# Two output products of a hybrid decoder layer by Strassen's method

## The chip, the cores and the metric

The kernel runs on one core of a Trainium2 chip. TensorE (PE) multiplies, VectorE (DVE), ScalarE (ACT) and GpSimd (POOL) do the rest, SyncE (SP) issues transfers. The metric is the device time of one execution in microseconds.

## What is computed

One layer over 512 tokens of 1024 channels, in float32: a SwiGLU FFN, a token mixer, a cross-attention into 256 memory tokens, and another FFN. Each is added to a scaled `h` and normalised. Cut to what matters here:

```python
def _swiglu(h, w_in, w_out):
    gate, up = jnp.split(h @ w_in, 2, axis=-1)
    return (jax.nn.silu(gate) * up) @ w_out          # w_out 2816 x 1024

def _parallel_mixer(h, w_in, lb, gnorm, pool_w, pool_scale, w_out):
    ...                                              # 4 HGRN2 heads -> o, 4 pooled groups -> p, each (.., 512, 512)
    merged = jnp.concatenate([o, p], axis=-1)
    return merged @ w_out                            # w_out 1024 x 1024

def _memory_attention(h, mem, wq, wk, wv, wo):
    ...                                              # 4 heads of 256
    o = jnp.einsum('bhsm,bmhd->bshd', p, v).reshape(b_, s_, D_MODEL)
    return o @ wo                                    # wo 1024 x 1024

h = _layernorm(ALPHA * h + 0.5 * _swiglu(h, w_ffn1_in, w_ffn1_out), ln1_g, ln1_b)
h = _layernorm(ALPHA * h + _parallel_mixer(h, ...), ln2_g, ln2_b)
h = _layernorm(ALPHA * h + _memory_attention(h, mem, ...), ln3_g, ln3_b)
h = _layernorm(ALPHA * h + 0.5 * _swiglu(h, w_ffn2_in, w_ffn2_out), ln4_g, ln4_b)
```

## The kernel before

**Float32 in three products.** Each operand of a product is split into a high part (a cast to fp32r) and a low part (the rest). `split` (L67, L68) does this: ACT casts, DVE subtracts. PE then runs high x high, high x low, low x high into one PSUM bank. `wblock` loads a block of weights (128 x 1024 float32, 512 KB: two contraction tiles of 512 output columns) into one of seven `raw` slots through SP's queue and splits it into `whi_` and `wlo_` (seven slots of tag `q` in all) or, for blocks that are kept, into one `ws_` tile.

**The two products in question.** `out_gemm` computes `merged @ w_out` (names `mo`, weights `wmixo`) and `o @ wo` (names `xo`). It goes over two halves of 512 output columns; in each, four weight blocks times four token tiles (128 tokens) times two contraction tiles times three parts. So 192 matmuls of 128x128 by 128x512 a product (L226, L227, L228), into a bank for each token tile. When a bank is done, DVE adds it to `alpha * h` (L243) and takes statistics (L246); in the second half the layer norm of that token tile follows (`ln_tile`: L173, L175, `rstd` on POOL L177, four DVE passes over half a tile each L180, L183), and `transpose_h` lets PE turn the normalised tile (`trh`, L195) and splits the turned tile into the next product's operand (`moT`, `xoT`). The bank of `trh` is one of two.

Their left sides come in already split: the gated heads of the mixer (`og`, L887) are split into `mg` for each of four stretches of 128 tokens, the pooled groups in `pool_out` (L735), the attention's outputs `po` in `values` into `oT`.

**The FFNs' second products** use `strassen_gemm`: one level of Strassen's method, with 2x2 blocks (two halves of tokens, two halves of the first 20 of 22 contraction tiles, two halves of output columns); seven products instead of eight. A product is `left` (split of a left quarter or of a combination of quarters), five weight blocks (`right`), 60 matmuls in `block` (L356) for two token tiles, and one to four additions of its banks `u`, `v`, `w` to `h` (`add`: L367 with the scale of `h`, L370 without). The combinations of left quarters are made by `combine` on DVE (L339). The combinations of right quarters (`t1` to `t4`) are made in DRAM by POOL's DMA queue: `Sums.copy` copies a block (L284), `Sums.add` adds another to it in flight (L293). `spread` issues 40 such actions for the second FFN behind 50 weight blocks, each behind a tiny POOL instruction (`seen`, L302) that reads the block's high part and so sets the time.

**Order.** Each engine runs its instructions in a written order, which a scheduler fixes when the kernel is built; an instruction that waits holds up all behind it on its engine. Behind the mixing product PE has keys (`pk`) and values (`vm`) of the memory to compute, which need no `h`; behind the attention product it starts the second FFN (`f2p`), which needs `xoT`.

Of the kernel before, what the change touches and what calls it, by code (L numbers as in the profile page):

```python
# [16 lines left out]
P = 128  # L17
S = 512
# [16 lines left out]
def layer_kernel(ctx: ExitStack, tc: tile.TileContext, a, out):  # L35
# [173 lines left out]
    def out_gemm(wsrc, nkt, act, alpha, g, b, eps, name, final=False, order=None, stay=4, ys=None, pre=None):  # L209
        nb = nkt // 2  # L210
        order = list(range(nb)) if order is None else order
        tiles = None
        stats = [st.tile([P, 2, 6], F32, tag=f"stats{t}", name=f"stats{t}", bufs=1) for t in range(NT)]
        for hf in range(2):
            ps = [None] * NT
            head = nb - (2 if hf == 0 else stay)

            def part(t, i, w):
                if ps[t] is None:
                    ps[t] = mm_ps(f"{name}ps{hf}{t}")  # L220
                hi, lo = w
                for j in range(2):
                    ah, al = act(order[i] * 2 + j)
                    tsl = slice(t * P, (t + 1) * P)
                    wh, wl = hi[:, j * 512:(j + 1) * 512], lo[:, j * 512:(j + 1) * 512]
                    nc.tensor.matmul(ps[t], ah[:, tsl], wh, start=i == 0 and j == 0, stop=False)  # L226
                    nc.tensor.matmul(ps[t], ah[:, tsl], wl, start=False, stop=False)  # L227
                    nc.tensor.matmul(ps[t], al[:, tsl], wh, start=False, stop=i == nb - 1 and j == 1)  # L228

            for i in range(head):  # L230
                w = wblock(wsrc[hf, order[i]], f"{name}{hf}_{i}")
                for t in range(NT):
                    part(t, i, w)
            ws = [wblock(wsrc[hf, order[i]], f"{name}{hf}_{i}", stay=hf == 1 and i < head + 3) for i in range(head, nb)]
            if hf == 1:
                GB = ln_bcast(g, b)
                if pre is not None:
                    pre()
            for t in range(NT):
                for i, w in enumerate(ws):  # L240
                    part(t, head + i, w)
                sl = slice(hf * 512, hf * 512 + 512)
                nc.vector.scalar_tensor_tensor(  # L243
                    out=h[t][:, sl], in0=h[t][:, sl], scalar=float(alpha), in1=ps[t],
                    op0=ALU.mult, op1=ALU.add)
                nc.vector.bn_stats(stats[t][:, hf, :], h[t][:, sl])  # L246
                if hf == 1:
                    ln_tile(t, stats[t], GB, eps)
                    if final:
                        for q in range(2):  # L250
                            nc.sync.dma_start(out[t * P:(t + 1) * P, q * 512:(q + 1) * 512], h[t][:, q * 512:(q + 1) * 512])
                    else:
                        if t == 0:
                            tiles = [quarter(f"{name}T{q}") if ys is not None else b8([P, 2, 2, S], F32R, f"{name}T{q}")
                                     for q in range(4)]
                        transpose_h(t, tiles, ys)
        if final:
            return None
        if ys is not None:
            return tiles  # L260
        return [(tiles[k // 2][:, k % 2, 0, :], tiles[k // 2][:, k % 2, 1, :]) for k in range(KT)]

    KB1, KB2 = [0, 1, 4, 5, 8], [2, 3, 6, 7, 9]
    NB = len(KB1)

    class Sums:


        def __init__(self, wsrc, name):
            self.w, self.name, self.T = wsrc, name, {}
            self.copies = [(p, b) for b in range(NB) for p in ("t1", "t3", "t2", "t4")]
            self.adds = list(self.copies)

        def copy(self, behind, of=("t1", "t3", "t2", "t4"), engine=None):

            todo = [c for c in self.copies if c[0] in of]
            if todo:
                p, b = todo[0]  # L280
                self.copies.remove(todo[0])
                T = self.T[p, b] = scr.tile([P, 1024], F32, name=f"{self.name}{p}{b}")
                with tc.issue_after(behind):
                    (engine or nc.sync).dma_start(T, self.w[p in ("t3", "t2"), (KB2 if p in ("t2", "t4") else KB1)[b]])  # L284

        def add(self, behind):

            if self.adds and self.adds[0] in self.T:
                p, b = self.adds.pop(0)
                x = {"t1": lambda: self.w[1, KB1[b]], "t3": lambda: self.w[1, KB2[b]],  # L290
                     "t2": lambda: self.T["t1", b], "t4": lambda: self.T["t2", b]}[p]()
                with tc.issue_after(behind):
                    nc.gpsimd.dma_start(self.T[p, b], x, accum_op=ALU.add, max_dma_last_dim=8192)  # L293

        def spread(self, hi, over, count=[0]):

            total = 8 * NB
            n0, n1 = (total * (count[0] + i) // over for i in range(2))
            count[0] += 1
            for n in range(n0, min(n1, total)):  # L300
                seen = st.tile([P, 1], F32, tag="seen", name="seen")
                ins = nc.gpsimd.tensor_tensor(out=seen, in0=hi[:, 0:1].bitcast(F32), in1=mhalf[:, 0:1], op=ALU.mult).ins  # L302
                if self.copies and (n % 2 == 0 or n < 4):
                    self.copy(ins, engine=nc.gpsimd)
                else:
                    self.add(ins)

        def step(self, q, n):
# [5 lines left out]
            for _ in range(3 if n < 4 else 2):  # L314
                self.copy(ins, engine=nc.gpsimd)

    def strassen_gemm(wsrc, gt, S_, alpha, g, b, eps, name, final, pre):
        tiles = None
        stats = [st.tile([P, 2, 6], F32, tag=f"stats{t}", name=f"stats{t}", bufs=1) for t in range(NT)]
        lo, hi = slice(0, 256), slice(256, 512)  # L320
        quarter_ = {n: [gt[i][:, :, sl], gt[i + 2][:, :, sl], gt[4][:, i:i + 2, sl]]
                    for n, i, sl in (("a11", 0, lo), ("a12", 1, lo), ("a21", 0, hi), ("a22", 1, hi))}
        for n, i, sl in (("a12", 2, lo), ("a22", 2, hi)):
            quarter_[n][2] = gt[4][:, i:i + 2, sl]
# [12 lines left out]
        def combine(o, x, y, op):  # L337
            for i in range(3):
                nc.vector.tensor_tensor(out=quarter_[o][i], in0=quarter_[x][i], in1=quarter_[y][i], op=op)  # L339

        def right(p, stay=0):

            direct = {"b11": (0, KB1), "b21": (0, KB2), "b22": (1, KB2)}
            for i in range(NB):
# [14 lines left out]
        def product(T, p, ps, opens):  # L359
            for i, w in enumerate(right(p)):  # L360
                for t in range(2):
                    block(t, i, w, T, ps[t], opens, False)
# [12 lines left out]
        s1 = b8([P, 2, 4, 256], F32, f"{name}s1")  # L375
        s1_ = sm.tile([P, 2, 256], F32, tag="s1", name=f"{name}s1_", bufs=2)
        quarter_["s1"] = [s1[:, 0], s1[:, 1], s1_]
# [15 lines left out]
        product(L, "b21", w, True)  # L393
        combine("a12", "a12", "a11", ALU.add)
        L = left("a12")

        T = b8([P, 2, 2, S], F32R, f"{name}gs")
        split(gt[5][:, :2, :], T[:, :, 0, :], T[:, :, 1, :])
        gs = [[(T[:, k, 0, sl], T[:, k, 1, sl]) for k in range(2)] for sl in (lo, hi)]
        product(L, "b22", v, False)  # L400
# [665 lines left out]
```

## Time and profile before

| what | value |
|---|---|
| median of 3 runs | 1042.48 us (1042.39 to 1042.53) |
| profiled execution | 1043.13 us, span 1041.4 us |
| PE busy | 1025.7 us (98%) |
| DVE busy | 825.4 us (79%) |
| ACT busy | 504.3 us (48%) |
| POOL busy | 95.0 us (9%) |
| mean granted clock | 0.997 |

A row of instructions gives start, busy time, engine, line, operation and output<-inputs, shape and count; a bracket tells how long the engine was idle before it and what released it. A group has no start, and gives after the bar busy time and the mean ns of one, then idle time before them. A row of a stretch gives its bounds, its length and the busy time of PE, of the weight loads, DVE, ACT and POOL (with counts), then the granted TensorE clock, the share of the DMA engines and GB/s. Matmuls are pipelined, so that their durations overlap: what one costs is the step to the next start.

### The profile page before, as it was taken

The page shows a single profiled execution, that of the slowest core. Times are in us where ns is not written, and L with a number is a line of the kernel's source. Part 1 is how long each engine was busy: PE and PEld are TensorE (multiplying, and loading weights), DVE is VectorE, ACT ScalarE, POOL GpSimd, SP SyncE. Part 2 cuts the span into 40 slices and gives each one's busy share as a digit, 9 for nine tenths or more (in the row PEclk, how much of TensorE's full clock was granted, in tenths as well). Part 3 has the DMA queues.
Part 4 walks back from the last instruction along what each step waited for, and adds up shares of the span by engine and source line. Part 5 has one row for each costly group of instructions (what it writes and reads, how often), then busy time and mean ns, then how long its engine had stood idle before and what let it go on. Part 6 is the DMA issues. An engine that isn't in the chain of part 4 may idle for free. (4 is left out here: it accounts for less than half of the span.)

```text
span 1041.4 us, 17704 instructions
## 1 busy us (share of the span) xinstructions
PE 1025.7 (98%) x6910; PEld 929.4 (89%) x6910; DVE 825.4 (79%) x1334; ACT 504.3 (48%) x857; POOL 95.0 (9%) x167
## 2 busy tenths in 40 slices
PE   9999999999999999999999999999999999999996
PEld 7999999998887888879888988889999999988884
DVE  6999888789898545786786356589988888889795
ACT  5656555566554331334324345226555555566530
POOL 0112211200000111102303110010000000000000
PEclk9999999999999999999999999999999999999998
DMA  9377786585665446553929871403233332436751
GB/s 364 143 236 230 222 254 212 148 247 158 216 192 182 142 155 169 148 168 82 292 72 314 273 162 41 141 22 107 97 101 122 103 101 65 139 102 202 235 189 41
DMA packets 43300, 171.59 MB, mean 165 GB/s; under 512 B 6096, under 2 KB 7376, under 8 KB 40016
## 3 DMA queue, kind: packets, MB, share of 16 engines
q1 hardware_dynamic: 38592, 128.25, 36.9%
q0 software_dynamic: 4480, 41.95, 15.9%
q8 instruction: 54, 0.88, 0.3%
q10 hardware_dynamic: 144, 0.26, 0.1%
q14 instruction: 30, 0.25, 0.1%
HBM read 168.34 MB, written 44.04 MB: 204 GB/s over the span
## 5 line engine op out<-in xcount | busy, mean ns | idle before, releaser
L177 POOL TENSOR_TENSOR rstd<-ve,mhalf 128x1 f32<-128x1 f32 x16 | 14.8, 922 | 536.1 <-DVE ve L175 536.1
L538 PE MATMUL f1u<-xt,qf1s 128*128 128x256 f32 x480 | 60.7, 283 | 0.0
L538 PE MATMUL f2u<-xt,qf2s 128*128 128x256 f32 x480 | 60.7, 283 | 0.0
L538 PEld LDWEIGHTS f1u<-xt,qf1s 128*128 128x128 f32 x480 | 59.0, 192 | 0.0
L538 PEld LDWEIGHTS f2u<-xt,qf2s 128*128 128x128 f32 x480 | 59.0, 192 | 0.0
L68 DVE TENSOR_TENSOR wlo_wv<-raw_wv,whi_wv 128x1024 fp32r<-128x1024 f32 x12 | 14.7, 1224 | 23.8 <-PE pq L57 8.5
L538 PE MATMUL f1u<-xT,qf1a 128*128 128x256 f32 x240 | 32.1, 283 | 0.0
L538 PE MATMUL f2w<-xoT,qf2a 128*128 128x256 f32 x240 | 32.1, 283 | 0.0
L538 PE MATMUL f2u<-xoT,qf2a 128*128 128x256 f32 x240 | 32.1, 283 | 0.0
L538 PE MATMUL f1w<-xT,qf1a 128*128 128x256 f32 x240 | 32.1, 283 | 0.0
L538 PE MATMUL f1v<-xt,qf1s 128*128 128x256 f32 x240 | 30.7, 283 | 0.0
L538 PE MATMUL f1u<-xt,qf1a 128*128 128x256 f32 x240 | 30.6, 283 | 0.0
L538 PE MATMUL f1v<-xT,qf1s 128*128 128x256 f32 x240 | 30.4, 283 | 0.0
L538 PE MATMUL f2v<-xt,qf2s 128*128 128x256 f32 x240 | 30.4, 283 | 0.0
L538 PE MATMUL f2v<-xoT,qf2s 128*128 128x256 f32 x240 | 30.4, 283 | 0.0
L538 PE MATMUL f2u<-xt,qf2a 128*128 128x256 f32 x240 | 30.4, 283 | 0.0
L538 PEld LDWEIGHTS f1w<-xT,qf1a 128*128 128x128 f32 x240 | 30.3, 192 | 0.1
L538 PEld LDWEIGHTS f1u<-xT,qf1a 128*128 128x128 f32 x240 | 30.2, 192 | 0.0
L538 PEld LDWEIGHTS f2w<-xoT,qf2a 128*128 128x128 f32 x240 | 30.2, 192 | 0.0
L538 PEld LDWEIGHTS f2u<-xoT,qf2a 128*128 128x128 f32 x240 | 30.2, 192 | 0.0
L538 PEld LDWEIGHTS f1v<-xt,qf1s 128*128 128x128 f32 x240 | 29.6, 192 | 0.1
L538 PEld LDWEIGHTS f1u<-xt,qf1a 128*128 128x128 f32 x240 | 29.6, 192 | 0.0
(458 smaller groups left out, 3220.3 us busy)
## 6 DMA issues: line engine op xcount, KB each, us to landing
f1t<-in_w1out POOLq DMA_DIRECT2D x30, 512.0 KB, 8.2
f2t<-in_w2out POOLq DMA_DIRECT2D x30, 512.0 KB, 6.6
raw_f1t<-f1t SPq DMA_DIRECT2D x20, 512.0 KB, 4.1
raw_f2t<-f2t SPq DMA_DIRECT2D x20, 512.0 KB, 3.9
raw_f2g<-in_w2in SPq DMA_DIRECT2D x17, 512.0 KB, 3.7
raw_f2u<-in_w2in SPq DMA_DIRECT2D x17, 512.0 KB, 3.7
raw_f1u<-in_w1in SPq DMA_DIRECT2D x15, 512.0 KB, 7.2
raw_f1b<-in_w1out SPq DMA_DIRECT2D x15, 512.0 KB, 4.8
```

What stands on the lines that cost most here:

```text
L68: nc.vector.tensor_tensor(out=lo, in0=src, in1=hi.bitcast(F32), op=ALU.subtract)
L177: nc.gpsimd.tensor_tensor(out=rstd, in0=ve, in1=mhalf[:, 0:1], op=ALU.pow)
L538: nc.tensor.matmul(o, q[:, w, wsl], x[k][r], start=opens and k == 0 and n == 0, stop=ends and k == 3 and n == 2, skip_group_check=True)
```

## The change

`strassen_gemm` takes any list of groups of left tiles (three for an FFN, one for the others), with or without the last two contraction tiles, and computes `mo` and `xo` as well; `out_gemm` goes. With one group a product has two weight blocks and 24 matmuls. The heads, pooled groups and attention outputs stay plain float32 (`mgh`, `mgp`, `oT`), and their splits go; `left` splits quarters and combinations (`moa`, `mos`, `xoa`, `xos`). `Sums` makes the right sums of both products too, on POOL's queue, and instead of `spread` one action of the list `todo_behind` is issued behind each weight block from the Q projection to the attention product (16 for `mo`, then 16 for `xo` in turn with 40 for the second FFN).

```diff
-    def out_gemm(wsrc, nkt, act, alpha, g, b, eps, name, final=False, order=None, stay=4, ys=None, pre=None):
...
     class Sums:
-        def __init__(self, wsrc, name):
+        def __init__(self, wsrc, name, kb1, kb2):
...
+        def actions(self):
+            n = len(self.copies)
+            return [x for i in range(n + 4) for x in ([self.copy] if i < n else []) + ([self.add] if i >= 4 else [])]
...
+    def one_behind(hi):
+        if todo_behind:
+            seen = st.tile([P, 1], F32, tag="seen", name="seen")
+            todo_behind.pop(0)(nc.gpsimd.tensor_tensor(out=seen, in0=hi[:, 0:1].bitcast(F32), in1=mhalf[:, 0:1],
+                                                       op=ALU.mult).ins)
+
+    def strassen_gemm(groups, last_two, S_, alpha, g, b, eps, name, final=False, pre=None, ys=None):
...
-    def strassen_gemm(wsrc, gt, S_, alpha, g, b, eps, name, final, pre):
-        tiles = None
...
+        quarter_ = {n: [x[i][:, :, sl] for x in groups]
                     for n, i, sl in (("a11", 0, lo), ("a12", 1, lo), ("a21", 0, hi), ("a22", 1, hi))}
...
         def combine(o, x, y, op):
-            for i in range(3):
+            for i in range(len(groups)):
                 nc.vector.tensor_tensor(out=quarter_[o][i], in0=quarter_[x][i], in1=quarter_[y][i], op=op)
...
+        if len(groups) == 1:
+            quarter_["s1"] = [raw4([P, 4, 256], f"{name}s1")]
...
-            tiles = [b8([P, 2, 2, S], F32R, f"{name}T{q}") for q in range(4)]
+            tiles = [quarter(f"{name}T{q}") if ys is not None else b8([P, 2, 2, S], F32R, f"{name}T{q}") for q in range(4)]
             for t in range(2):
-                transpose_h(t, tiles)
+                transpose_h(t, tiles, ys)
...
-    behind.append(lambda hi: sums2.spread(hi, 50))
+    sums_mo, sums_xo = Sums(a["wmixo"], "mo", [2, 3], [0, 1]), Sums(a["wo"], "xo", [0, 1], [2, 3])
+    todo_behind += sums_mo.actions()
+    todo_behind += [x for two in zip(sums_xo.actions(), sums2.actions()) for x in two]
+    todo_behind += sums2.actions()[len(sums_xo.actions()):]
+    behind.append(one_behind)
...
-        mh, ml = mslot(4 + g)
-        nc.scalar.activation(mh, pm, AF.Copy, scale=psc[:, g:g + 1])
-        nc.vector.scalar_tensor_tensor(out=ml, in0=pm, scalar=psc[:, g:g + 1], in1=mh.bitcast(F32),
-                                       op0=ALU.mult, op1=ALU.subtract)
+        nc.scalar.activation(mg[1][:, g, :], pm, AF.Copy, scale=psc[:, g:g + 1])
...
-        ov = og.rearrange("p (a b n) -> p a b n", a=2, b=2)
-        for q in range(2):
-            split(ov[:, q], mg[q][:, :, 0, cs], mg[q][:, :, 1, cs])
-
-    X2 = out_gemm(a["wmixo"], KT, mslot, ALPHA, a["ln2_g"], a["ln2_b"], LN_EPS, "mo", order=[2, 3, 0, 1])
+    X2 = strassen_gemm([(mg[1], mg[0])], None, sums_mo, ALPHA, a["ln2_g"], a["ln2_b"], LN_EPS, "mo")
...
-            split(po, oT[:, j, 0, :], oT[:, j, 1, :])
+            nc.scalar.copy(out=OT[hd // 2][:, 2 * (hd % 2) + j, :], in_=po)
...
-    X3 = out_gemm(a["wo"], KT, lambda k: (OT[k // 2][:, k % 2, 0, :], OT[k // 2][:, k % 2, 1, :]),
-                  ALPHA, a["ln3_g"], a["ln3_b"], LN_EPS, "xo", ys=ys,
-                  pre=lambda: wx.extend(wblock(a["w2in"][u * FT], f"f2{'gu'[u]}0") for u in range(2)))
+    X3 = strassen_gemm([OT], None, sums_xo, ALPHA, a["ln3_g"], a["ln3_b"], LN_EPS, "xo", ys=ys,
+                       pre=lambda: wx.extend(wblock(a["w2in"][u * FT], f"f2{'gu'[u]}0") for u in range(2)))
```

In the changed kernel the lines of `strassen_gemm` and `Sums` stand some 50 higher: combines L280, matmuls L297, additions to `h` L308 and L311, statistics L362, copies and adds in DRAM L225 and L234, `seen` L256, heads L831. The seven products are, in order, `b11` and `t1` (banks `mou`, `mov`), `t2` (`mou`), `b21` (`mow`), `b22` (`mov`), `t3` and `t4` (`mou`); numbers behind a name tell tiles apart, and `h_266` to `h_269` are the four token tiles.

Where the orders change, first on DVE at the start of the mixing product. Before, the last gated heads and the low parts of weights:

```order
L887 SCALAR_TENSOR_TENSOR og<-ot,gn,GS 128x512
L68 TENSOR_TENSOR ws_mo_0_5486<-raw_mo_0_5484,ws_mo_0_5486 128x1024
L68 TENSOR_TENSOR mg_5147<-og,mg_5147 128x2x128
L68 TENSOR_TENSOR mg_5148<-og,mg_5148 128x2x128
L68 TENSOR_TENSOR wlo_mo_3_5422<-raw_mo_3_5419,whi_mo_3_5421 128x1024
L68 TENSOR_TENSOR ws_mo_1_5495<-raw_mo_1_5493,ws_mo_1_5495 128x1024
```

Now, from the last gated heads to the weights of the second product and beyond:

```order
L831 SCALAR_TENSOR_TENSOR mgh<-ot,gn,GS 128x4x128
L280 TENSOR_TENSOR mos_5338<-mgp,mgh 128x1024
L280 TENSOR_TENSOR mgp<-mgp 128x4x256
L68 TENSOR_TENSOR mos_5384<-mos_5338,mos_5384 128x4x256
L308 SCALAR_TENSOR_TENSOR h_266<-h_266,mou_5329 128x512
L308 SCALAR_TENSOR_TENSOR h_267<-h_267,mou_5330 128x512
L68 TENSOR_TENSOR wlo_mot_5392<-raw_mot_5389,whi_mot_5391 128x1024
L68 TENSOR_TENSOR wlo_mot_5414<-raw_mot_5411,whi_mot_5413 128x1024
L280 TENSOR_TENSOR mgp<-mos_5338,mgp 128x4x256
```

The low part of the second product's first weights (`wlo_mot_5392`) stands behind two combinations, a left split and the additions of the first product. Next, the end of the same product, on PE, where now the transposes of two tiles and the last product (`ws_mot_5662`) mix:

```order
L297 MATMUL mou_5330<-whi_mot_5638,moa_5591 128x512
L195 MATMUL trh_5682<-ident,h_266 128x128 x4
L195 MATMUL trh_5691<-ident,h_266 128x128 x4
L56 MATMUL pk<-mT_5011,whi_wk_5808 128x256
L57 MATMUL pk<-mT_5011,whi_wk_5808 128x256
L297 MATMUL mou_5329<-ws_mot_5662,moa_5657 128x512
L195 MATMUL trh_5700<-ident,h_267 128x128 x4
```

and on DVE, ahead of the subtraction that reads the bank `mou_5329` before the last product may write it:

```order
L180 SCALAR_TENSOR_TENSOR h_266<-h_266,mv,G 128x512 x2
L173 BN_AGGR mv<-stats_5326 128x2
L68 TENSOR_TENSOR moa_5657<-mgh,moa_5657 128x4x256
L183 SCALAR_TENSOR_TENSOR h_266<-h_266,rstd,B 128x512 x2
L175 TENSOR_SCALAR ve<-mv 128x1
L180 SCALAR_TENSOR_TENSOR h_267<-h_267,mv,G 128x512 x2
L183 SCALAR_TENSOR_TENSOR h_267<-h_267,rstd,B 128x512 x2
L68 TENSOR_TENSOR ws_mot_5662<-raw_mot_5660,ws_mot_5662 128x1024
L68 TENSOR_TENSOR wlo_mot_5671<-raw_mot_5668,whi_mot_5670 128x1024
L68 TENSOR_TENSOR moT_5678<-trh_5682,moT_5678 128x2x128
L311 TENSOR_TENSOR h_268<-h_268,mou_5329 128x512
```

Before, the same place on PE went from one token tile's matmuls to the next tile's, each with a bank of its own, and one tile's transposes between them:

```order
L195 MATMUL trh_5561<-ident,h_266 128x128 x4
L195 MATMUL trh_5570<-ident,h_266 128x128 x4
L226 MATMUL mops_5579<-whi_mo_3_5508,mg_5148 128x512
L227 MATMUL mops_5579<-wlo_mo_3_5509,mg_5148 128x512
L228 MATMUL mops_5579<-whi_mo_3_5508,mg_5148 128x512
```

So two whole norms and two low parts of weights now stand ahead of the last product's bank. Last, POOL in the attention product, where before the last add of the second FFN's sums was issued behind the product's second weight block, well ahead of the first `rstd`, and where now stands:

```order
L234 DMA f2t_6897<-f2t_6575 64x2048
L256 TENSOR_TENSOR seen<-ws_xot_7160,mhalf 128x1
L225 DMA f2t_7165<-in_w2out 16x8192
L256 TENSOR_TENSOR seen<-whi_xot_7169,mhalf 128x1
L234 DMA f2t_6947<-f2t_6897 64x2048
L177 TENSOR_TENSOR rstd<-ve,mhalf 128x1 x2
```

`f2t_6947` is added from `f2t_6897`, and so waits until that block's own add has landed; the `rstd` of the first two tiles stands behind it.

More of the change, by code (lines that the diff above doesn't have):

```diff
@@ L392, in strassen_gemm @@
             add(t, 1, u[t], True, ALU.subtract)
-        product(L, "b21", w, True)
+        product(L, "b21", w, True, last_two is None)
         combine("a12", "a12", "a11", ALU.add)
         L = left("a12")
[L397 to L400, printed above, removed]
-        ws = [wblock(wsrc[hf, 2 * NB], f"{name}{hf}_{2 * NB}", stay=True) for hf in range(2)]
+        if last_two is not None:
+            T = b8([P, 2, 2, S], F32R, f"{name}gs")
+            split(last_two, T[:, :, 0, :], T[:, :, 1, :])
+            gs = [[(T[:, k, 0, sl], T[:, k, 1, sl]) for k in range(2)] for sl in (lo, hi)]
+        product(L, "b22", v, False, last_two is None)
+        if last_two is not None:
+            ws = [wblock(wsrc[hf, 2 * nb], f"{name}{hf}_{2 * nb}", stay=True) for hf in range(2)]
         GB = ln_bcast(g, b)
@@ L411, in rest @@
         def rest(t, hf, ps, opens, scale):
-            block(t % 2, 0, ws[hf], gs[t // 2], ps, opens, True)
-            add(t, hf, ps, scale)
+            if last_two is not None:
+                block(t % 2, 0, ws[hf], gs[t // 2], ps, opens, True)
+            if ps is not None:
+                add(t, hf, ps, scale)
             nc.vector.bn_stats(stats[t][:, hf, :], h[t][:, hf * 512:hf * 512 + 512])
@@ L851, in layer_kernel @@
         states.append(Sn)
-    for q in range(2):
-        mg[q] = b8([P, 2, 2, S], F32R, f"mg{q}")
+    mg[0] = b8([P, 4, S], F32, "mgh")
     os_ = []
```

138 lines of the change are left out of this document (36 added, 102 removed).

## Prediction

> **What bounds the kernel now.** I read the page first, then the stretches of the two stages that change, then single rows of PE and DVE.
>
> ```profile
> span 1041.4 us, 17704 instructions
> PE 1025.7 (98%) x6910; PEld 929.4 (89%) x6910; DVE 825.4 (79%) x1334; ACT 504.3 (48%) x857; POOL 95.0 (9%) x167
> ```
>
> PE is the bound almost without a gap, so a matmul less is time less, as long as PE stays the bound. That must be asked stage by stage. The next rows are the mixing product with the `pk` and `vm` work behind it, the attention product, and twenty microseconds of the first FFN's Strassen stage:
>
> ```profile
> core 0: us, PE busy (x) PEld busy (x) DVE busy (x) ACT busy (x) POOL busy (x), PEclk, DMA share, GB/s
> 494.11:542.16 48.05, 48.02 (x227) 38.92 (x225) 36.51 (x63) 13.68 (x26) 11.01 (x17) 1.00 0.61 186
> 647.98:697.20 49.22, 48.53 (x225) 39.66 (x224) 32.57 (x50) 13.32 (x18) 2.97 (x3) 1.00 0.24 76
> 250.00:270.00 20.00, 20.00 (x89) 16.54 (x89) 19.94 (x21) 14.17 (x16) 0.00 (x0) 1.00 0.58 189
> ```
>
> In both products DVE has 12 to 16 us to spare out of some 48. In the FFN's Strassen stage PE is full, but DVE has no slack at all (19.94 of 20.00). That third row is the warning. Where the two products and what follows them begin:
>
> ```profile
> 494.11 0.48 PE L226 MATMUL mops<-whi_mo,mg 128*128 128x512 f32 x1
> 542.16 0.28 PE L56 MATMUL pk<-mT,whi_wk 128*128 128x256 f32 x1
> 542.28 0.28 PE L57 MATMUL pk<-mT,whi_wk 128*128 128x256 f32 x1
> 557.51 0.40 PE L909 MATMUL vm<-whi_wv,mT 128*128 128x512 f32 x1
> 647.98 0.40 PE L226 MATMUL xops<-whi_xo,oT 128*128 128x512 f32 x1
> 697.74 0.28 PE L56 MATMUL f2p<-xoT,whi_f2g 128*128 128x256 f32 x1
> ```
>
> **PE: the matmuls removed.** Each stage had 8 blocks x 4 token tiles x 6 = 192 matmuls of 512 columns and gets 7 products x 24 = 168, so 24 fewer in each. A matmul's duration overlaps its neighbours', so its price is the step between starts:
>
> ```profile
> L226 PE MATMUL mops<-whi_mo,mg 128*128 128x512 f32 x40 | 16.0, 399 | 0.0
> 1022.69 5.60 PE L356 MATMUL f2u<-ws_f2t,f2a 128*128 128x512 f32 x24
> 1028.13 0.39 PE L356 MATMUL f2u<-whi_f2t,f2a 128*128 128x512 f32 x1
> 541.23 0.63 PE L195 MATMUL trh<-ident,h 128*128 128x128 f32 x4
> 541.61 0.48 PE L227 MATMUL mops<-wlo_mo,mg 128*128 128x512 f32 x1
> ```
>
> 24 matmuls take 1028.13 - 1022.69 = 5.44 us, 0.227 each (not the 0.399 of the group row). So a product costs PE 5.44 us, and the work removed is 24 x 0.227 = 5.44 us a stage, **-10.9 us** together. Four transposes take 541.61 - 541.23 = 0.38.
>
> **DVE: what a product costs it.** Prices, again as steps between starts:
>
> ```profile
> 262.86 1.22 DVE L339 TENSOR_TENSOR f1g<-f1g,f1g 128x1024 f32<-128x1024 f32 x1
> 264.00 1.22 DVE L68 TENSOR_TENSOR wlo_f1t<-raw_f1t,whi_f1t 128x1024 fp32r<-128x1024 f32 x1
> 265.13 1.22 DVE L339 TENSOR_TENSOR f1g<-f1g,f1g 128x1024 f32<-128x1024 f32 x1
> 271.56 1.28 DVE L367 SCALAR_TENSOR_TENSOR h<-h,f1u 128x512 f32<-128x512 f32 x2
> 272.75 1.22 DVE L68 TENSOR_TENSOR wlo_f1b<-raw_f1b,whi_f1b 128x1024 fp32r<-128x1024 f32 x1
> 304.14 0.69 DVE L415 BATCH_NORM_STATS2 stats<-h 128x6 f32<-128x512 f32 x1
> 304.75 0.67 DVE L370 TENSOR_TENSOR h<-h,f1v 128x512 f32<-128x512 f32 x1
> 309.91 1.41 DVE L180 SCALAR_TENSOR_TENSOR h<-h,mv,G 128x512 f32<-128x512 f32 x2
> 311.23 1.41 DVE L183 SCALAR_TENSOR_TENSOR h<-h,rstd,B 128x512 f32<-128x512 f32 x2
> 495.04 1.40 DVE L887 SCALAR_TENSOR_TENSOR og<-ot,gn,GS 128x512 f32<-128x512 f32 x2
> 496.36 0.75 DVE L68 TENSOR_TENSOR mg<-og,mg 128x256 fp32r<-128x256 f32 x2
> ```
>
> A combine or a low part of 128x1024: 1.135. An add of a PSUM bank to `h`: 0.60. Statistics: 0.61. A normalising pass over half a tile: 0.66. A head gating: 0.66. A Strassen product thus asks DVE for two block low parts and a left low part (3.4 us), and on the average half a combine and two adds (1.8): 5.2 us beside PE's 5.44, before any layer norm. In the FFNs the same left side and adds spread over five blocks:
>
> ```profile
> 998.37 13.60 PE f2u L356 x60
> ```
>
> 60 matmuls in 13.60 us there, 24 in 5.44 here. Adds, combines of the full 1024 columns and the norms do not shrink with the two blocks. I therefore take DVE to be the bound of both stages, and walk its order.
>
> *Mixing product.* DVE's row order from the first head gating to the first `h_268 -= mou` holds 12 block low parts (13.6), 7 left low parts (7.9), 4 combines (4.5), 11 adds (6.6), 4 statistics (2.4), 8 normalising passes (5.3), 4 gatings (2.6) and small ones (1.5): **44.4 us**. It starts when the heads are ready, at 494.7, as before: 539.1. Over the same stretch PE has six products and few transposes: 6 x 5.44 + 0.8 = 33.4, which would end at 527.5. PE must lose the difference, 11 to 12 us, since the first matmul of the last product writes the bank that this subtraction reads. Where: in small pieces at product 2 (its first low part stands behind two combines, a left split and two adds) and at the first transposes (behind the norm), and some 5 us in one piece ahead of the last product, behind two whole layer norms. Then follow on PE 5.44 for that product, six groups of transposes (2.3), 118 `pk` matmuls at 0.12 (14.2), and short waits for the last two tiles' norms and for a late `wk` block, which I put at 3.4 (0 to 5). 539.1 + 5.4 + 2.3 + 14.2 + 3.4 = 564.4 for the first `vm`, which stood at 557.5: **+7** (floor, with no wait after 539.1: +3.5).
>
> The removed low parts (8 of the gated heads, 4 of the pooled groups) are in that sum already, by their absence; so are the casts of ACT, which has 34 of 48 us free.
>
> *Attention product.* DVE cannot begin the first combine before the last head is copied, about 648.9. From there to the first `h_268 -= xou` it has 12 block low parts (13.6), 6 left (6.8), 4 combines (4.5), 11 adds (6.6), 4 statistics (2.4), 8 passes (5.3) and small ones (1.1): 40.3 us. It waits some 1.1 for the end of product 1 (648.0 + 5.4) and, by my walk, about 2 more: 692. PE, free at 648.0 + 33.4 = 681.4, waits 10 to 11 in all, some 6 of it in one piece. Then 5.4 + 0.8 of transposes, and up to 1 for a transposing bank: 699.1 against 697.7, with two groups of transposes (0.8) left over that before stood ahead: +2.2. Put beside it POOL:
>
> ```profile
> 560.85 0.80 POOL L293 DMA_DIRECT2D f2t<-f2t  x1 [4.36 <-DMA f2t<-f2t]
> 680.83 1.00 POOL L177 TENSOR_TENSOR rstd<-ve,mhalf 128x1 f32<-128x1 f32 x1 [59.70 <-DVE ve L175]
> f2t<-f2t POOLq DMA_DIRECT2D x10, 512.0 KB, 8.0
> raw_mo<-in_wmixo SPq DMA_DIRECT2D x8, 512.0 KB, 4.0
> ```
>
> Before, POOL had been idle 59.70 us when the norm asked for `rstd`. Now a chained add stands ahead of the first two `rstd`, and it may be issued only when the add it builds on has landed (8.0 us after its issue; such a wait was 4.36 before). The bound is 0 to 8 us late; since the other add is issued several microseconds ahead of the norm, I take 1. Attention stage: **+3** (0 to +10).
>
> *Second FFN's start.* DVE still has the last two tiles' norms and their sums to do while PE wants weights: **+0.5** (0 to +2).
>
> *DMA and the sums.* 32 more POOL transfers and 12 more block loads of 512 KB in all. The loads are issued blocks ahead and land in about 4 us; the mixing stage moves 186 GB/s at a share of 0.61, so I cost them at nothing. What hides them is the seven raw slots; if the slots come free too late (they do so on DVE's low part), a load of 4 us shows, up to about 5 us a stage. SP only gets more issues. The right sums of the second FFN finish later than before but an FFN's length ahead of their use.
>
> **Sum.** +7 + 3 + 0.5 = +10.5 on a profiled execution of 1043.13 (span 1041.4) is 1053.6; the median of the runs is 1042.48, 0.65 less: **1053.0**.
>
> **The clock.** After PE's last matmul (at about 1031) the granted clock read:
>
> ```profile
> 1032.00:1035.00 3.00, 0.00 (x0) 0.00 (x0) 2.93 (x7) 0.00 (x0) 0.92 (x1) 1.00 0.00 0
> 1035.00:1038.00 3.00, 0.00 (x0) 0.00 (x0) 0.54 (x1) 0.00 (x0) 0.00 (x0) 0.60 0.45 175
> ```
>
> A mean of 0.60 over 1035 to 1038 between 1.00 and 0.50 puts the fall near 1035.6, 4.6 us into the pause. My two long waits are 5 to 6 us, just past it. If the clock stays at half for as long as it took to fall, PE loses 2.3 us after each: +4.6 at most. My waits are so near that edge that I leave this out of the sum and keep it as a rival. The Trainium skill's page "TensorE: Matmul & The Clock Gate", Part 1, says that the array halves its clock after one idle window of about 3.4 us and wants as long of work to recover. By that rule the loss would be about 1.7 us a wait, +3.4, an estimate from its figure. The trace agrees that a fall comes (0.60 in the row above), and has no such pause inside the kernel to show the recovery.
>
> **Rivals.**
> - *PE stays the bound, DVE fits*: the full -10.9, 1031.6. For it speaks the FFN stage, with both engines full; against it the 44.4 us of DVE against PE's 33.4. It decides if a 128x1024 operation took under about 0.65 us instead of 1.135, or if the waits fell where PE has other work. 7 in 100.
> - *One stage's loss is smaller*: the attention product loses no wait (-5.4) and the mixing one +7: 1044, no change to speak of. 5 in 100.
> - *The clock falls in both waits*: 1056 to 1057.5. 13 in 100.
> - *POOL or the loads come late*: `rstd` up to 8 late, or blocks 5 a stage: 1058 to 1063. 12 in 100.
> - *The forecast*: DVE is the bound of both stages, 1049 to 1056. 63 in 100.
>
> Below 1047 lie the first two (12 in 100), above 1061 a part of the fourth (some 4); so the range is 1047 to 1061. Two thousandths (2.1 us) is about what this kernel's runs can tell from no change: faster 0.08, same 0.05, slower 0.87.
>
> **What would show it.** Right: in the mixing and attention products DVE near 100% busy and PE 75 to 80%; waits of PE on `h` (L311), on the transposing bank and on low parts, one of some 5 us in each stage; `vm` starting near 564. Wrong: PE without gaps there (DVE cheaper than its rows), or waits on DMA or POOL in front.

## The result and the profile after

The changed kernel took 1074.68 us (median of 4, 1073.15 to 1075.97) against 1042.43 (1041.41 to 1042.53): a ratio of 1.0311, 95% interval 1.0293 to 1.0329. The forecast was 1053.0, range 1047 to 1061: the direction was right, the size a third of what came. The profiled execution took 1073.15, its page begins:

```profile
span 1071.3 us, 17784 instructions
PE 1028.6 (96%) x6862; PEld 928.7 (87%) x6862; DVE 857.7 (80%) x1360; ACT 526.6 (49%) x875; POOL 128.9 (12%) x230
```

48 matmuls fewer, and yet PE is busy 2.9 us longer. The stretches of the two stages show why (columns as before; the clock is the third figure from the right). The first runs to the first matmul of the mixing product's last Strassen product, the second to the first `vm`, the third from the last `po` to the first `f2p`:

```profile
494.88:540.92 46.04, 36.42 (x158) 27.80 (x156) 42.95 (x54) 19.81 (x22) 16.31 (x28) 0.97 0.85 277
540.92:569.40 28.48, 26.52 (x166) 24.64 (x167) 24.35 (x45) 12.74 (x25) 10.92 (x16) 0.86 0.78 246
662.20:724.09 61.89, 48.05 (x186) 37.56 (x185) 48.86 (x63) 25.71 (x30) 19.63 (x31) 0.83 0.80 233
```

PE is busy 79% of the first and 78% of the third stretch, where it had been without a gap. DVE is near full in the first, but not in the third. And two things stand there that before did not: a clock of 0.97, 0.86 and 0.83, and a DMA share of 0.80 in the attention product, which had 0.24. What PE waited for most in the whole kernel (total, times, longest):

```profile
PE trh L195 <- DVE h L183: 5.9, 3, 3.7
PE trh L195 <- ACT y L206: 5.0, 1, 5.0
PE mou L297 <- DVE h L311: 3.9, 1, 3.9
PE xou L297 <- ACT whi_xot L67: 2.7, 1, 2.7
PE xov L297 <- DVE wlo_xot L68: 1.9, 1, 1.9
PE mov L297 <- DVE wlo_mot L68: 1.5, 1, 1.5
```

The waits are those that the prediction named: norms, the transposing bank, the subtraction `h` (L311), low parts. One more is a weight block's high part. Where they come from is read from DVE and ACT. First the mixing product, DVE:

```profile
525.69 1.23 DVE L68 TENSOR_TENSOR wlo_mot<-raw_mot,whi_mot 128x1024 fp32r<-128x1024 f32 x1 [2.21 <-ACT whi_mot L67]
540.19 0.68 DVE L311 TENSOR_TENSOR h<-h,mou 128x512 f32<-128x512 f32 x1
```

The subtraction that frees the last product's bank stands at 540.19; the walk had 539.1. So DVE's order did bound this stretch, with a late block of 2.2 us in it. Then the attention product, three rows of DVE and two of ACT, with the times from issue to landing of these blocks (`raw_xot`, least, median, most) and, last, those of the same weights before (`raw_xo`):

```profile
691.25 0.68 DVE L362 BATCH_NORM_STATS2 stats<-h 128x6 f32<-128x512 f32 x1
699.05 1.22 DVE L68 TENSOR_TENSOR wlo_xot<-raw_xot,whi_xot 128x1024 fp32r<-128x1024 f32 x1 [7.11 <-ACT whi_xot L67]
708.21 1.42 DVE L183 SCALAR_TENSOR_TENSOR h<-h,rstd,B 128x512 f32<-128x512 f32 x2 [2.96 <-POOL rstd L177]
697.03 1.04 ACT L67 CAST ws_xot<-raw_xot 128x1024 fp32r<-128x1024 f32 x1 [8.87 <-DMA raw_xot<-xot]
697.98 1.04 ACT L67 CAST whi_xot<-raw_xot 128x1024 fp32r<-128x1024 f32 x1
DMA to landing us min/median/max: 3.1/10.2/15.5
DMA to landing us min/median/max: 4.0/4.3/11.9
```

DVE stood still for 7.1 us in the middle of its 40 us of work, because blocks of right sums landed 10 to 15 us after their issue instead of 4; and for 3.0 us more because `rstd` stood behind an add in POOL's queue. The block that DVE lacked, the second of t3, was not the last to land. The next two rows are the landings of the blocks issued at 680.3 and 681.5:

```profile
DMA to landing us min/median/max: 11.0/11.0/11.0
DMA to landing us min/median/max: 15.5/15.5/15.5
```

The t3 block was there at 691.3 (680.3 + 11.0), when DVE came to want it. In ACT's order the first block of t4 (`ws_xot`) stands ahead of it: ACT waited for that one until 697.0 (681.5 + 15.5), and the t3 block's cast came behind it without a wait of its own (the row at 697.98). So most of the 7.1 us is a late block of the next product, passed on by ACT's order; no run changed that order. POOL's queue moved this much in the whole kernel (packets, MB, share; before: 4480 packets, 15.9%):

```profile
q0 software_dynamic: 6272, 58.73, 21.6%
```

Last, the clock. After a wait of PE of 1.9 us for product 2 of the attention product:

```profile
668.00:669.00 1.00, 0.52 (x3) 0.09 (x1) 1.00 (x2) 0.34 (x1) 0.00 (x0) 1.00 1.72 524
669.00:670.00 1.00, 0.00 (x0) 0.00 (x0) 1.00 (x2) 1.00 (x2) 0.00 (x0) 1.00 0.00 0
670.00:671.00 1.00, 0.58 (x3) 0.49 (x4) 1.00 (x2) 1.00 (x2) 0.19 (x1) 1.00 0.45 74
671.00:675.00 4.00, 4.00 (x12) 3.18 (x11) 3.94 (x4) 3.44 (x4) 3.62 (x5) 0.59 1.04 313
675.00:676.00 1.00, 1.00 (x5) 0.79 (x4) 0.01 (x1) 0.10 (x1) 0.00 (x0) 0.94 0.92 188
699.00:705.00 6.00, 5.47 (x12) 3.76 (x12) 5.95 (x10) 1.06 (x2) 2.81 (x5) 0.50 0.88 241
```

PE is busy from 671 on, at half the clock for some 3.4 us: 12 matmuls in 4 us, where at 0.227 a step 17 fit. The same shows from 538 to 545, 562 to 565, 699 to 705 and 709 to 719.

These falls have an order. All five begin and end on one grid of 3.41 us, and each follows a step of the grid in which PE stood still for 1.9 us or more. The first two rows are such a step and the one behind it; the last two, from the later run `e10_light_filled`, are the two steps over which a pause of 2.2 us was spread, 0.8 and 1.4 us, and nothing fell:

```profile
668.31:671.72 3.41, 1.51 (x7) 1.08 (x7) 3.41 (x5) 3.06 (x4) 0.91 (x2) 1.00 0.81 239
671.72:675.13 3.41, 3.41 (x10) 2.67 (x9) 3.23 (x3) 2.83 (x3) 2.90 (x4) 0.50 1.06 309
700.50:703.91 3.41, 2.60 (x12) 1.80 (x10) 3.41 (x6) 0.28 (x1) 0.77 (x1) 1.00 0.42 154
703.91:707.32 3.41, 2.06 (x11) 1.77 (x12) 3.26 (x7) 2.19 (x5) 0.00 (x0) 1.00 0.53 154
```

In the traces of all thirteen kernels, the change and the later runs included, every step at full clock with 1.9 us or more of idle time is followed by half clock and none with 1.6 us or less; in between both occur.

A count of every microsecond gives the whole: PE's idle time, and its busy time times what the clock lacked of 1.00. Mixing stage (first `ot` to first `vm`): 12.4 idle + 3.9 lost to the clock; attention product (last `po` to first `f2p`): 13.8 + 7.2; before, 0.7 in all. Together 36.6 us more, less the 10.9 of removed matmuls: 25.7 of the 29.9 by which the span grew. 2.6 stand behind PE's last matmul: 13.4 us to the end of the span, where it had been 10.8. The 1.6 left over were not followed. The count says where PE's time went; why it went is what the runs below ask.

### The profile page after: what moved, and what is told of

Read it like the earlier page. It is cut to its first block, busy times and chain, and to the rows that moved or that the text cites. A ratio compares the mean times of both kernels' runs of the same rounds, so it can differ in the third digit from the quotient of the medians.

```text
span 1071.3 us, 17784 instructions
## 1 busy us (share of the span) xinstructions
PE 1028.6 (96%) x6862; PEld 928.7 (87%) x6862; DVE 857.7 (80%) x1360; ACT 526.6 (49%) x875; POOL 128.9 (12%) x230
```

## The experiments

All times are medians; "before" ran beside each. Theory A was that DVE bounds both stages, with late weights and the clock on top; its rivals are in the quoted expectations. Of each edit only the lines that matter are shown.

**One product at a time** (`e1_mo_only`, `e2_xo_only`): the other one is computed by `out_gemm` as before.

```diff
-    X3 = strassen_gemm([OT], None, sums_xo, ALPHA, ...
+    X3 = out_gemm(a["wo"], KT, lambda k: (OT[k // 2][:, k % 2, 0, :], OT[k // 2][:, k % 2, 1, :]), ALPHA, ...
```

> The mixing product by Strassen as changed, the attention product as before; 56 actions on the right sums instead of 72, done before the attention product's third weight block. Theory A (in each of the two stages VectorE's order is too long for the shorter products, and late weights and a falling clock come on top): the first vm stands 9 to 12 us later than before, the attention stage as before, 1051 to 1055 us in all. Rival B (the transfers of the sums, not VectorE, hold the stages up): the mixing stage has nearly the same transfers, so it loses as much, but with waits on weight blocks in front. Rival C (the loss comes from the two stages acting on one another, above all from sums that slip into the attention stage): under 1046.

> The attention product by Strassen as changed, the mixing product as before; 56 actions, some 8 of them still in the attention stage where the change has 14. Theory A: the attention stage loses 3 to 6 us from VectorE's order alone and up to 10 more from late weights and the late rstd: 1047 to 1056. Rival B: the loss of the attention stage is made by the sums' transfers there, with half as many it falls to about half, 1048 to 1050, and the wait for the high part of a t3 block (7.1 us) goes. Rival C (both stages lose only together): under 1045.

Measured: 1058.24 (ratio 1.0150, 1.0135 to 1.0165) and 1052.59 (1.0094, 1.0077 to 1.0111): +15.6 and +9.9. Each loses by itself, so rival C falls, though some 7 of the change's 32 us come only with both together. With the mixing product alone the first `vm` comes 13.4 us later than before, more than expected; the attention product alone loses 8.9 us in its stage instead of 14.9. Theory A's range was missed by the first run and met by the second; B's 1048 to 1050 was missed.

**The transfers moved out of the two stages** (`e3_sums_early`): two actions behind each block elsewhere, none inside.

```diff
+        if quiet[0]:
+            return
+        for _ in range(min(2, len(todo_behind))):
             seen = st.tile([P, 1], F32, tag="seen", name="seen")
```

> All as changed, the whole result computed, but two actions on the right sums behind each weight block outside of the two products and none inside them. Theory A (VectorE's order bounds both stages and the late weights are an addition in the attention stage): the 7.1 us wait for a t3 block, the 3.0 us for rstd and part of the low clock go, 15 to 20 us less than the change, 1055 to 1060; PE still waits on VectorE in both stages. Rival B (the transfers are the whole cause): under 1045. Rival D (the low clock after each wait is most of it): time falls only as far as pauses over 1 us go; 1060 to 1068.

Measured: 1072.65 (1.0282, 1.0262 to 1.0302), only 2.0 less: missed by all three. The trace shows why. The attention product lost its late block and its late `rstd` and fell from 61.9 to 50.0 us; but the projections ahead of it, which had hidden everything, took 102.1 us instead of 92.8. There the DMA engines now had no room (DMA share 1.02 over 60 us). PE waited 1.7 us for weights and 3.6 on the softmax (`pt`), and lost clock. DVE, which makes what `pt` needs, had stood up to 7 us at POOL's tiny `seen`, which reads a weight slot that is wanted again and itself stood behind chained adds:

```profile
567.70:628.00 60.30, 58.61 (x308) 50.93 (x307) 19.77 (x21) 17.51 (x22) 20.05 (x41) 0.97 1.02 309
PE pt L901 <- DVE e L893: 3.6, 2, 3.4
622.46 1.22 DVE L68 TENSOR_TENSOR wlo_wxq<-raw_wxq,whi_wxq 128x1024 fp32r<-128x1024 f32 x1 [6.95 <-POOL seen L258]
```

**DVE's low parts left out** (`e4_no_lows`).

```diff
-        split(raw, hi, lo)
+            nc.scalar.copy(out=hi, in_=raw)
+            nc.vector.tensor_tensor(out=lo[:, :8], in0=raw[:, :8], in1=hi[:, :8].bitcast(F32), op=ALU.subtract)
+            lo = hi
```

> As changed, but in the two products the low parts are left out on VectorE: each subtraction is cut to 8 columns, and PE multiplies the high part in its place, so that PE's matmuls, the casts, the loads and the sums' transfers are the same; some 24 us of VectorE work less in each stage. Theory A: PE is the bound of the mixing stage again and wins there (vm 3 to 5 us earlier than before the change); in the attention stage the late weights remain: 1045 to 1055. Rival B (transfers): hardly better than the change, over 1065. If VectorE is the whole cause: about 1032 to 1036.

Measured: 1068.01 (1.0244, 1.0228 to 1.0259), where rival B had it (over 1065). DVE is busy 815.1 us instead of 857.7, some 21 less in each stage, and that brought 6.7. So theory A in that form fell too: with DVE relieved, late blocks of right sums decided. In the mixing product ACT waited 12.1 us for one of t3. In the attention product DVE stood 4.9 and 6.1 us for the two of t4, whose low parts stand ahead of the norm in its order, and PE waited 13.2 us for that norm:

```profile
523.87 1.04 ACT L85 CAST whi_mot<-raw_mot 128x1024 fp32r<-128x1024 f32 x1 [12.11 <-DMA raw_mot<-mot]
707.80 1.94 PE L202 MATMUL trh<-ident,h 128*128 128x128 f32 x8 [13.22 <-DVE h L190]
```

This gave theory E: two holdups side by side, and taking away one lets the other decide. It asks for both, singly and together, without moving the transfers where they hurt.

**Transfers made light** (`e6_light`): the second FFN's sums made inside that FFN, where its `step` takes what is left; nothing inside the two products. And **both** (`e7_light_no_lows`): the same with the low parts left out.

```diff
-    todo_behind += [x for two in zip(sums_xo.actions(), sums2.actions()) for x in two]
-    todo_behind += sums2.actions()[len(sums_xo.actions()):]
+    todo_behind += sums_xo.actions()
```

> All as changed and the whole result computed, but the second FFN's right sums are made inside that FFN (as the first FFN's are), and no action of the sums stands inside the two products: 32 actions behind other blocks. Theory E (two holdups stand side by side in both stages, VectorE's order and weight blocks made late by the sums' transfers; taking one away lets the other decide): now VectorE's order decides alone, the first vm comes 8 to 10 us later than before, the attention stage loses 2 to 4 us, the end 2 to 3 us: 1053 to 1058. Rival B (transfers are the cause): under 1046. Rival F (VectorE and transfers are both minor, the falling clock is the cause): over 1062.

> The kernel with the second FFN's sums moved, and in the two products the low parts left out on VectorE (each cut to 8 columns; PE multiplies the high part instead). Theory E: with both holdups gone PE bounds both stages, -5.4 us each, +0.8 for transposes and 2 to 3 at the end: 1034 to 1038. Rival G (a third wait stands behind, such as the layer norms or the bank of the last product): over 1042, with that wait in front of PE.

Measured: 1064.44 (1.0214, 1.0199 to 1.0229) and 1049.88 (1.0077, 1.0062 to 1.0092), both above what theory E gave. The first lies where rival F had it (over 1062), the second where rival G had it; rival B falls. Against the change, leaving out the low parts brings 6.7 us, light transfers 10.2, both together 24.8: more than the sum, as theory E has it. F, by which both are minor, does not fit that. The stages (us, from the starts of the same matmuls in each trace; the profiled execution of e7 took 1052.12, 2.2 above its median):

| | before | change | lows out (e4) | light (e6) | both (e7) |
|---|---|---|---|---|---|
| mixing, first `ot` to first `vm` | 64.2 | 77.0 | 76.4 | 74.8 | 68.9 |
| attention product, last `po` to first `f2p` | 47.0 | 61.9 | 55.9 | 51.0 | 41.4 |
| first `f2p` to first `f2w` | 24.4 | 25.3 | 27.2 | 25.3 | 27.1 |
| second FFN, `f2w` to last `f2u` | 308.5 | 308.5 | 308.5 | 312.4 | 313.8 |
| behind the last matmul | 10.8 | 13.4 | 13.3 | 13.4 | 13.3 |

In the attention product theory E holds: with both away it takes 41.4 us, 5.6 less than before, near the 5.44 of removed matmuls, with PE full at a clock of 1.00 (first row). Two groups of transposes have moved behind the first `f2p`, though, and PE waits 1.5 there; up to the first `f2w` the gain is 2.9. With the transfers light and DVE whole the stage takes 51.0, and now DVE is full and PE is not (second row). Blocks land in 3.2 us again (third, of this run).

```profile
654.70:696.10 41.40, 40.59 (x186) 33.28 (x185) 28.27 (x58) 24.71 (x29) 1.98 (x2) 1.00 0.53 178
659.80:710.80 51.00, 43.50 (x186) 35.00 (x185) 48.99 (x64) 25.54 (x30) 2.59 (x3) 0.93 0.48 154
DMA to landing us min/median/max: 3.1/3.2/6.1
```

In the mixing stage a part stays. With both away the product itself runs from 495.1 to 537.2, 5.7 us less than before, but the last tiles' norms then hold PE, as rival G had it, and the clock falls behind these waits (3.6 us lost there):

```profile
545.97 0.79 PE L202 MATMUL trh<-ident,h 128*128 128x128 f32 x4 [2.39 <-DVE h L190]
548.43 1.08 PE L202 MATMUL trh<-ident,h 128*128 128x128 f32 x4 [1.67 <-DVE h L190]
```

Missed by both expectations: the second FFN pays 4 to 5 us for making its own sums, and the clock, which by the same count takes 4.4 and 2.8 us of `e6_light`'s two stages.

**GpSimd for the weights' low parts** (`e8_light_pool_lows`).

```diff
+            nc.gpsimd.tensor_tensor(out=lo, in0=raw, in1=hi.bitcast(F32), op=ALU.subtract)
```

> The kernel with the second FFN's sums moved, and the 14 low parts of weight blocks in each of the two products computed by GpSimd instead of VectorE; the whole result is computed. Theory E: if such an operation takes GpSimd under 2 us, VectorE loses 15.9 us of 44.4 and PE is nearly the bound: 1038 to 1046. If GpSimd takes over 3 us for one, the low parts and rstd come late: over 1055. Rival G: no better than the kernel without this, whatever GpSimd takes.

Measured: 1075.45 (1.0315, 1.0298 to 1.0332), the second branch, and no better than without, as rival G had it too. One takes 2.95 us on the mean, the starts of the blocks on PE are 3.34 apart, and PE waits 0.3 to 1.8 us for most of them. The mean hides two sizes (fourth row, least, median, most in ns): some 2.40 us, and 3.38 where DVE works beside it on two inputs of that size. And DVE's own operation of 128x1024, 1.2 us where no such subtraction runs, took 2.1 to 3.4 us beside one (last row):

```profile
L86 POOL TENSOR_TENSOR wlo_mot<-raw_mot,whi_mot 128x1024 fp32r<-128x1024 f32 x7 | 20.5, 2948 | 8.0 <-ACT whi_mot L85 8.0
503.06 0.50 PE L306 MATMUL mov<-wlo_mot,mos 128*128 128x512 f32 x1 [1.26 <-POOL wlo_mot L86]
506.40 0.50 PE L306 MATMUL mov<-wlo_mot,mos 128*128 128x512 f32 x1 [0.55 <-POOL wlo_mot L86]
L86 POOL TENSOR_TENSOR wlo_mot<-raw_mot,whi_mot x7: 2397/2845/3382, 500.5 to 533.8; 128x1024 fp32r<-128x1024 f32 x7
507.35 3.42 DVE L68 TENSOR_TENSOR moa<-mgh,moa 128x1024 fp32r<-128x1024 f32 x1
```

**A bank of its own for the last product** (`e9_light_own_bank`).

```diff
-                block(t, i, x, L, u[t], False, last_two is None and i == nb - 1)
+                block(t, i, x, L, u[t] if last_two is not None else w[t], last_two is None, last_two is None and i == nb - 1)
```

> The kernel with the second FFN's sums moved, and the last product of the two Strassen stages (t4) accumulating in the banks of w, free by then, so that it need not wait for the subtraction from h; two more additions of 0.60 us on VectorE in each stage. Theory E: PE's wait on that subtraction (3.5 to 5 us in the mixing stage) goes, but VectorE's work is the same and 1.2 longer, so that most of it comes back at the last norms: 0 to 3 us less than without. Rival H (that one wait, with the clock that falls in it, is the loss of the mixing stage): 6 to 9 us less.

Measured: 1072.66 (1.0299, 1.0270 to 1.0328), 8.2 more than `e6_light`. Rival H falls: PE's wait on the subtraction went, and one of 4.2 us took its place: on the low part of that product's first block, which stands behind the same norms on DVE. The profiled execution was the slowest of the four (1077.53). In it the mixing stage takes 78.8 us instead of `e6_light`'s 74.8, the stretch from the last `po` to the first `f2w` 80.5 instead of 76.4, the second FFN 317.2 instead of 312.4. Why was not followed.

```profile
PE mow L297 <- DVE ws_mot L68: 4.2, 1, 4.2
```

**The pauses filled** (`e10_light_filled`): 16 idle matmuls where PE waits longest.

```diff
+                if t == 0 and last_two is None:
+                    for i in range(16):
+                        nc.tensor.matmul(w[0], L[0][0][:, :P], T4[0][0][:, :512], start=True, stop=True, ...
```

> The kernel with the second FFN's sums moved, and 16 more matmuls (3.6 us, into a bank that is free, result not used) in each of the two products, placed in PE's order between the last product's predecessor and the last product, where PE waits 4.9 and 5.6 us on VectorE. The result is the same. If the clock falls because of these waits: the filled pauses fall below 2.5 us, the granted clock stays at 1.00 there, and the 4.4 + 2.8 us lost to it while busy go: 5 to 7 us less than without the filling (1057 to 1060). If the low clock is not from the pauses, or costs nothing on the path: the same as without, or up to 2 us more.

Measured: 1066.94 (1.0248, 1.0230 to 1.0265), 2.5 more than `e6_light`: neither branch. In the attention product it did what was expected: the pause of 5.6 us became 2.2, the clock stayed at 1.00, the 2.8 us lost to it went to 0 and the stage from 51.0 to 48.4.

```profile
699.63 3.47 PE L381 MATMUL xow<-ws_xot,xoa 128*128 128x512 f32 x14
705.26 0.66 PE L195 MATMUL trh<-ident,h 128*128 128x128 f32 x4 [2.16 <-ACT y L206]
```

In the mixing stage 2.8 us of pause were left, the clock fell all the same, and the later norms waited longer (77.6 us for 74.8). From the first `f2p` to the last `f2u` it took 1.6 us more than `e6_light`. So filling a pause held the clock in one of two places; what the clock costs in all was not taken away by a run, only counted.

**The transfers by themselves** (`e11_sums_only`): both products by `out_gemm`, all the right sums made and not used.

```diff
+    todo_behind += sums_mo.actions()
+    todo_behind += [x for two in zip(sums_xo.actions(), sums2.actions()) for x in two]
```

> The products as before the change, but all the right sums of both are made as in the change (72 actions behind weight blocks, 32 more than before) and not used. Theory E: without Strassen's additional blocks and with VectorE's slack the transfers are mostly hidden; the end is 2.5 us longer (0.08 us for each of 32 more actions, as the runs so far show after the last output): 1044 to 1048. Rival B (the transfers alone cost most of the 32 us): over 1055. Rival I (the longer end is not the actions'): the end as before, 10.8 us behind PE's last matmul.

Measured: 1045.92 (1.0042, 1.0027 to 1.0057), as theory E had it: rival B falls. 13.4 us stand behind PE's last matmul, with the old products. With 80, 96, 96, 112 and 112 actions on POOL's queue (before, e1, e2, this, the change) the end is 10.8, 12.0, 12.0, 13.4 and 13.4: 0.08 us an action. What runs there the trace does not show.

**Attention product alone, its left low parts on GpSimd** (`e12_xo_pool_left`): the try at a version that wins.

```diff
+                    nc.gpsimd.tensor_tensor(out=t[:, :, 1, :], in0=x, in1=t[:, :, 0, :].bitcast(F32), op=ALU.subtract)
```

> The mixing product as before; the attention product by Strassen, no action of the sums inside it, and its seven left low parts computed by GpSimd (some 3 us each) instead of VectorE; the whole result is computed. Theory E: VectorE keeps 32.4 of 40.3 us against PE's 33.4, the attention stage gains 2 to 4 us, given back in part by the end (+1.2) and two later transposes (+0.9): 1039 to 1043. If the other wait (low part of product 2 behind the combines) or GpSimd decides: 1044 to 1050.

Measured: 1048.82 (1.0065, 1.0050 to 1.0080), the second branch. The stage takes 49.1, 2.1 more than before, and the stretch from the first `f2p` to the first `f2w` 3.3 more. Product 2 still waits for its low part behind two combines, and the clock falls behind that wait. The second of these combines (third row) took 3.29 us where the first took 1.22, with one of GpSimd's subtractions beside it (second row). Five of DVE's operations of that size stand beside one in this trace and take 2.8 to 3.4 us, some 9 us more than at their old price, where the seven low parts moved had saved 7.9. The expectation had counted on the old price:

```profile
652.06 1.22 DVE L340 TENSOR_TENSOR oT<-oT 128x1024 f32<-128x1024 f32 x1
653.19 2.41 POOL L332 TENSOR_TENSOR xos<-xos,xos 128x1024 fp32r<-128x1024 f32 x1 [2.50 <-ACT xos L331]
653.39 3.29 DVE L340 TENSOR_TENSOR oT<-xos,oT 128x1024 f32<-128x1024 f32 x1
658.47 0.50 PE L357 MATMUL xov<-wlo_xot,xos 128*128 128x512 f32 x1 [1.98 <-DVE wlo_xot L68]
660.00:665.00 5.00, 5.00 (x18) 3.99 (x18) 5.00 (x2) 2.59 (x3) 4.00 (x2) 0.74 0.59 202
```

No version tried beats the kernel before.

## Why the prediction fell short

The forecast added 7 us for the mixing stage, 3 for the attention stage and 0.5 behind it. Measured were 11.9 (first `vm`), 14.9 and 1.0, and 2.6 at the end. The attention stage is the miss.

- *PE: -5.44 us a stage.* Right, and shown where little else holds: 41.4 for 47.0 in `e7_light_no_lows`.
- *DVE bounds both stages.* Right as far as it went. Its walk ended at 539.1 in the mixing product (540.2 measured), in part by luck: two of its four gatings (1.3 us) had run before 494.9, and waits of 3.0 us in all, which it did not have, more than made up for them. In the attention product it ended at 692. `e6_light`, where the blocks are not late, begins this stage 9.1 us later and has the subtraction at 700.96 and PE going on at 701.7: 691.9 and 692.6. The walk's 48.4 us for that stage (699.1 less 650.7) is what `e10_light_filled` took with the clock at 1.00. That DVE's work is a cause and not only a sight, e6 against e7 shows: 9.6 us in that stage.
- *"The loads are issued blocks ahead and land in about 4 us ... I cost them at nothing."* This step failed. It took the landing time of the trace of before, where the attention product's DMA share was 0.24, for a stage in which the change itself puts 14 actions of POOL's queue and six more loads. The blocks of t3 and t4 landed there 9.5 to 15.5 us after their issue, and DVE stood 7.1 us at one place. ACT, with free time to spare, did not help: in its order it stood 8.9 us at one late block with the block that DVE lacked behind it. e3 and e6, which take the actions out of that stage, bring it from 61.9 to 50.0 and 51.0.
- *rstd, 1 us late.* DVE stood 3.0 us for it, within the bound of 0 to 8; mis-sized.
- *The clock, left out of the sum.* Failed. The edge was read off one pause at the kernel's end (4.6 us), which had begun within a step of the grid that was busy for 2.25 of its 3.41 us; inside the kernel half clock followed pauses of 1.9, 2.7 and 4 us, and it cost 11.1 us of PE's busy time. The Trainium skill's page "TensorE: Matmul & The Clock Gate", Part 1, has the fall after at least one idle window of about 3.4 us. The trace agrees with the half clock and with that length (the grid of 3.41 us), not with 3.4 us as a pause that is safe up to there: 1.9 us within a window were enough.
- *The second FFN's start, +0.5.* The term was for waits behind the last norms, and in the change PE has none from the first `f2p` to the first `f2w`. That this stretch is 1.0 longer is the two groups of transposes that moved there, which the prediction had put into the attention stage (0.8). So the size is near by luck.
- *The end.* Not thought of: 2.6 us.
- *The rivals.* They were set up as alternatives with 13 and 12 in 100, and both came, because late blocks make waits and waits make low clock. Their sum, not one of them, was the upper end: 10 us of late loads and `rstd`, 11 of the clock and 2.6 of the end on the forecast's 1053 give 1076.6, near the 1074.7. That is a rough count, since waits side by side do not simply add.

## What to carry to other kernels

Before work is taken off a full engine, add up per stage what the other engines must do in the time that is left, and then what the new transfers do to the landing times there: a landing time read from a stage with a quarter of the DMA engines in use is no price for one with four fifths. Where two holdups stand side by side, removing either alone shows little, and only the run without both tells what each was worth. A wait of a few microseconds on TensorE can cost more than its length: 1.9 us brought 1.7 us of lost clock behind it. And work moved from VectorE to GpSimd is no pure gain where both work on the same sizes side by side: each slowed the other.

## What the runs showed of the hardware

- The clock went by steps of 3.41 us. It fell to half behind every step at full clock with 1.9 us or more of idle time of PE and behind none with 1.6 us or less; so a pause of 1.9 us within one step (668.5 to 670.4) was followed by half clock, and one of 2.2 us over two (703.1 to 705.3 in `e10_light_filled`) was not. Each fall lasted 3.4 us or more.
- Each action on POOL's queue lengthened the end of the kernel, behind the last output, by 0.08 us.
- Blocks of 512 KB landed 9.5 to 15.5 us after their issue beside POOL's copies and adds (DMA share 0.80), in a median of 3.2 without them (`e6_light`, 0.48).
- A subtraction of 128x1024 took GpSimd 2.40 us by itself and 3.38 beside VectorE's operations of that size; VectorE, which starts one every 1.135 us alone, took 2.1 to 3.4 us for one beside GpSimd's (`e8_light_pool_lows`, `e12_xo_pool_left`).
